# A hybrid conv/S5 layer on one core: state-space loads placed behind named weight loads, the conv matmuls, gelu and LayerNorm at other slots

## The chip, the cores and the metric

One core of a Trainium2 chip runs the whole kernel. The metric is the time of one launch in microseconds on the device. TensorE is called PE here, VectorE DVE, ScalarE ACT, GpSimd POOL, SyncE SP. "SPq" is SP's instruction queue, which issues nearly all DMAs; POOL issues the rest.

## The reference, cut to what matters

One layer is computed for 256 new positions of one sequence and 8 positions of each of 8 samples, 320 tokens together, in float32.

```python
xn = rmsnorm(x, norm_mix)
proj = xn @ w_in                        # 2048 -> 3072: value, gate, s_in of 1024 each
u = c_val * sigmoid(c_gate)             # group A
up = concat([conv_buf, u])              # conv_buf: the 30 rows kept of each sample
y = depthwise_conv(up, conv_w) + conv_b # width 31, then LayerNorm over channels, silu
# group B: S5, 64 groups of 16 channels, 64 complex states each
hs = associative_scan(complex, bu)      # starts from the incoming state of each sample
y = Re(C hs) + D * u; y = gelu(y); y = y * sigmoid(y @ w_glu)
mix = concat([rmsnorm(yc), rmsnorm(ys)]) @ w_out
h = x + mix
h = h + (silu(hn @ w_ffn_gate) * (hn @ w_ffn_up)) @ w_ffn_down
```

The outputs are the final rmsnorm of h for both kinds of token, the last 30 conv input rows and the last S5 states.

## The kernel before, in words

**The main work.** Every product with a weight matrix runs as three matmuls on rounded parts: weight and activation are each split into hi and lo, and hi*hi, lo*hi and hi*lo are added up in PSUM. The weights pass through in 352 sub-units (subs). A sub is two blocks of 128 weight rows by 512 columns, which makes 24 matmuls of 128x128 on 320 columns (two row blocks, four column blocks, three products; lines 151 to 153). `emit_dma` (line 113) loads its 512 KB into one of 4 `raw` buffers, in one DMA for the S5 columns and in two of 256 KB where value and gate columns are taken together. `emit_prep` (line 122) makes `hi` on ACT (line 127) and `lo` on DVE (line 128); `lo` is the last reader, so it frees the raw buffer, and the load of sub i waits for `lo` of sub i-4. Subs 0 to 15 are the S5 part of the input projection, 16 to 47 its conv part, 48 to 55 the S5 GLU, 56 to 87 the output projection (the S5 half first, then the conv half), and the rest is the FFN.

**What sets the order.** The program is written out sub by sub, and every piece is written under `when(slot)`: the slot, in units of subs, is a priority, and a scheduler puts each engine's instructions into one fixed order from these priorities and its own model of when operands are ready. `run_slot(i)` (line 132) writes the load of sub i at slot i-9, the split at i-2 and the matmuls at i. All other work of the mixer is a table, `PLAN`, of (what, index, slot):

```python
P_POST = [24, 25.5, 27, 28.5, 30, 31.5, 33, 34.5]
P_CONV = [27, 30, 35, 34, 43, 42, 51, 54]
+ [("gelu", b, P_GELU + b / 2) for b in range(8)]
+ [("conv", b, P_CONV[b] - (0 if b in V_CONV else 2.2)) for b in range(8)]
```

On each engine the instructions then run strictly in that order. A DMA is an instruction of SP's queue as well: while it waits for a buffer, all that stands behind it on SP waits too.

**The conv.** `conv_chunk(c)` (line 357) handles 128 channels. It loads the samples' old rows `stn` into its only buffer (line 361), turns them on PE (line 368) and copies them beside the new rows in `ubuf`; it turns the rows that are kept (line 371), copies them to `uo` and stores them as outputs 2 and 5 (lines 374, 375); then four DMAs copy four shifted views of `ubuf` into `ub` (line 381), 316 KB each. At slot `P_CONV[c]` PE runs 32 matmuls on 256 columns (line 389) and 32 on 64 columns (line 393); the trace counts each of these float32 matmuls twice. Chunks 3 and 5 do their taps on DVE instead. `gelu`, `ln_mean` to `ln_end` (slots `P_GELU` and `P_LN`) follow; LayerNorm closes with the row factors that the conv half of the output projection needs (`rg` line 292, turned on PE at line 300, then `Rc` line 302 and `t` line 993).

**The S5 part.** `s5_load2` (line 471), called from `s5_params2` (line 579) at slot 4, issues the B matrices `braw` (lines 475, 476), the C matrices `cn` (477, 478) and the incoming states `ssn` (482), ahead of them a zero fill of the scratch `KTd` (588), and `load_taps` the conv taps `cwn` (237). `post` (line 1182) reads a Toeplitz tile `tst` back from `KTd` through POOL, makes `hbd` on ACT, and on PE runs 8 matmuls of line 803 and 8 of line 808 (16 and 16 as the trace counts them), whose result is stored to `yd` (814); `gelu` reads `yd` back as `yl` (842), eight DMAs for each half. The copy of the 22 rows of old conv state that output 5 keeps is one DMA (1191).

Of the kernel before, what the change touches and what calls it, by code (L numbers as in the profile page):

```python
# [8 lines left out]
F32 = mybir.dt.float32  # L9
F32R = mybir.dt.float32r  # L10
I32 = mybir.dt.int32
AF = mybir.ActivationFunctionType
# [11 lines left out]
P_CONV = [27, 30, 35, 34, 43, 42, 51, 54]  # L24
V_CONV = {3: 0.2, 5: 0.2}
P_GELU = 44
P_LN = 62
E_AT = {2: 0, 3: 1024}
PT_BUFS = 2
N_CBLK = 1  # L30

# [14 lines left out]
        + [("copy", 0, 65)])  # L46
# [8 lines left out]
PREP_AHEAD = 2  # L55
@with_exitstack
def kernel(ctx: ExitStack, tc: tile.TileContext,
# [46 lines left out]
    raws = {}  # L104
    hls = {}
# [7 lines left out]
    def emit_dma(i):  # L113
        g, k0 = subs[i]
        r = rawp.tile([128, 2, 512], F32, tag="raw", name="raw")
        for w, row0, col0, n, off in g.srcs:
            SP.dma_start(r[:, :, off:off + n],
                         w[row0 + k0 * 128:row0 + (k0 + 2) * 128, col0:col0 + n]
                         .rearrange("(k p) n -> p k n", p=128))
        raws[i] = r  # L120

# [10 lines left out]
    def run_slot(i):  # L132
        with when(i - DMA_AHEAD):
            emit_dma(i)
# [65 lines left out]
    def sm_tile(shape, name):  # L200
        return s5.tile(shape, F32, name=name, tag="sm", bufs=4)
# [33 lines left out]
    def load_taps():  # L235
        late["cwn"] = s5.tile([128, 1024], F32, tag="ww", name="cwn", bufs=VW)
        SP.dma_start(late["cwn"][:31], conv_w[0])
# [118 lines left out]

    def conv_chunk(c):
        u = us_.pop(c)
        traced.add(("conv", c))
        stn = convp.tile([120, 2, 128], F32, name="stn", bufs=1)  # L360
        SP.dma_start(stn, sc_dram[:, c * 128:(c + 1) * 128]
                     .rearrange("(h r) c -> r h c", h=2))
# [108 lines left out]
    def s5_load2():  # L471
        braw = s5.tile([128, 2, 32, 16], F32, tag="et", name="braw", bufs=ET)
        cn = [s5.tile([128, 8, 64], F32, name=f"cn{i}", tag="ww" if i else "et", bufs=VW if i else ET)
              for i in range(2)]
        SP.dma_start(braw[:, 0], ssm_B_re[0].rearrange("(q g) p c -> (g p) q c", g=2))
        SP.dma_start(braw[:, 1], ssm_B_im[0].rearrange("(q g) p c -> (g p) q c", g=2))
        SP.dma_start(cn[0], ssm_C_re[0].rearrange("(k g) c p -> (g c) k p", g=8))
        SP.dma_start(cn[1], ssm_C_im[0].rearrange("(k g) c p -> (g c) k p", g=8))
        stn = [[sm_tile([128, 128], f"ssn{r}{h}") for h in range(2)] for r in range(2)]
        for r, src in enumerate((state_ssm_re, state_ssm_im)):  # L480
            for h in range(2):
                SP.dma_start(stn[r][h], src[0].rearrange("b (q g) p -> b q (g p)", g=2)
                            [:, 16 * h:16 * h + 16, :])
        return braw, cn, stn
# [94 lines left out]
    def s5_params2():  # L579
# [3 lines left out]
        for c in Cblk:  # L583
# [4 lines left out]
        SP.dma_start(KTd[:, 8:15].rearrange("b s c n -> (s c) b n"),  # L588
                     z[:, None, :].to_broadcast([112, 8, 128]))
        braw, cn, stn = s5_load2()  # L590
# [22 lines left out]
        for r in range(2):  # L613
            ps = sx_tile([128, 2, 128])
            for h in range(2):
                T.transpose(ps[:, h, :], stn[r][h], ident)
            A.activation(st0[:, r].rearrange("p (h q) b -> p h b q", h=2),
                         ps.rearrange("p h (b q) -> p h b q", b=8), AF.Copy)
# [530 lines left out]
    with when(-1.5):  # L1149
        load_x(4)  # L1150
        load_params()
    x_block(0)
# [18 lines left out]

    def c_step(c):
        return c
# [8 lines left out]
    def post(b):  # L1182
# [6 lines left out]
                  cw=conv_weights, conv=conv_chunk, sample=lambda b: s5_sample_states(),  # L1189
                  states=lambda b: s5_states(), open_g=lambda b: open_g(),  # L1190
                  copy=lambda b: SP.dma_start(ncv_s[0, :, 0:22, :], state_conv[0, :, 8:30, :]))
# [66 lines left out]
```

## Time and profile before

| | before |
|---|---|
| median of 3 runs | 1426.7 us (1422.41 to 1427.59) |
| the profiled execution's own time | 1431.02 us |
| its span | 1428.9 us |
| PE busy | 1385.4 us, 97% of the span |
| DVE busy | 827.2 us, 58% |
| ACT busy | 554.1 us, 39% |
| mean granted PE clock over the span | 0.982 |
| DMA | 220.11 MB, 154 GB/s on average |

A granted clock of 1.00 is PE at 2.4 GHz, 0.50 is 1.2 GHz. In a row of the timeline the columns are the start in us, the time to the end of the last of the merged instructions, the engine and line, the operation, what it writes and reads, how many, and in brackets the idle time of the engine before them and what ended it. Matmuls overlap, so a stretch of them is measured from start to start.

### The profile page before, as it was taken

What the parts mean: (1) busy time and instruction counts of PE and PEld (TensorE: products, weight loads), DVE (VectorE), ACT (ScalarE), POOL (GpSimd) and SP (SyncE); (2) the same over time, 40 slices, a digit from 0 to 9 for tenths busy, and PEclk for the clock granted to TensorE, in tenths of its full rate; (3) what the DMA queues carried; (4) which work ended last, traced back from release to release, by engine and by line L of the source; (5) the groups of instructions that cost most, each with busy time, mean ns of one, the idle gap of its engine ahead of it and who ended that gap; (6) DMA issues with size and microseconds to landing.
All of it is one profiled execution on the core that took longest, in us unless ns stands there. A gap on an engine that the chain in (4) does not pass through costs nothing.

```text
span 1428.9 us, 24831 instructions
## 1 busy us (share of the span) xinstructions
PE 1385.4 (97%) x10226; PEld 1352.4 (95%) x10226; DVE 827.2 (58%) x1518; ACT 554.1 (39%) x807; POOL 30.3 (2%) x61
## 2 busy tenths in 40 slices
PE   9899997899999999999999999999999999999995
PEld 8899986888999999999999999999999999999995
DVE  6788998776887744435434444443444435444465
ACT  7434433355364433333333332333333233332232
POOL 0121010000000000000000000000000000000000
PEclk9999998999999999999999999999999999999998
DMA  8875565467443444444444444445444444454432
GB/s 243 224 163 143 161 166 169 124 133 220 161 160 108 159 141 149 154 148 148 150 152 154 149 148 148 148 148 157 153 148 148 148 149 149 156 181 148 148 133 74
DMA packets 146585, 220.11 MB, mean 154 GB/s; under 512 B 32377, under 2 KB 57529, under 8 KB 146328
## 3 DMA queue, kind: packets, MB, share of 16 engines
q1 hardware_dynamic: 143336, 208.50, 47.3%
q0 software_dynamic: 3136, 10.03, 2.9%
q8 instruction: 80, 1.31, 0.4%
q14 instruction: 33, 0.27, 0.1%
HBM read 201.04 MB, written 10.41 MB: 148 GB/s over the span
## 4 chain that ended last, share of the span: by engine, by line
PE 88%; DMA 5%; DVE 2%; SPq 2%; ACT 1%; issue 1%; ACTq 0%; DVEq 0%
PE mm L151 27%; PE mm L152 27%; PE mm L153 27%; DMA ub<-ubuf 2%; PE cx L389 2%; DMA raw<-in_w_in_dram 2%; DVE lo L128 1%; SPq L842 1%; SPq L381 1%; ACT hi L127 1%; PE sx L808 1%; PE sx L710 1%; DMA yl<-yd 0%; DMA stn<-in_state_conv_dram 0%; PE sx L803 0%
## 5 line engine op out<-in xcount | busy, mean ns | idle before, releaser
L128 DVE TENSOR_TENSOR lo<-raw,hi 128x1024 fp32r<-128x1024 f32 x352 | 430.4, 1224 | 439.8 <-ACT hi L127 439.4
L127 ACT ACTIVATE hi<-raw 128x1024 fp32r<-128x1024 f32 x352 | 372.4, 1059 | 670.7 <-PE mm L152 605.2
L151 PE MATMUL mm<-hn,hi 128*128 128x320 f32 x1408 | 434.7, 309 | 0.0
L152 PE MATMUL mm<-hn,hi 128*128 128x320 f32 x1408 | 434.6, 309 | 0.0
L153 PE MATMUL mm<-hn,lo 128*128 128x320 f32 x1408 | 431.0, 309 | 0.0
L151 PEld LDWEIGHTS mm<-hn,hi 128*128 128x128 f32 x1408 | 264.2, 188 | 0.1
L152 PEld LDWEIGHTS mm<-hn,hi 128*128 128x128 f32 x1408 | 264.3, 188 | 0.0
L153 PEld LDWEIGHTS mm<-hn,lo 128*128 128x128 f32 x1408 | 263.2, 188 | 0.0
L151 PE MATMUL mm<-aout,hi 128*128 128x320 f32 x704 | 217.4, 309 | 0.0
L152 PE MATMUL mm<-aout,hi 128*128 128x320 f32 x704 | 217.1, 309 | 0.0
L153 PE MATMUL mm<-aout,lo 128*128 128x320 f32 x704 | 214.7, 309 | 0.0
L152 PEld LDWEIGHTS mm<-aout,hi 128*128 128x128 f32 x704 | 132.2, 188 | 0.0
L151 PEld LDWEIGHTS mm<-aout,hi 128*128 128x128 f32 x704 | 132.2, 188 | 0.0
L153 PEld LDWEIGHTS mm<-aout,lo 128*128 128x128 f32 x704 | 131.5, 188 | 0.0
L151 PE MATMUL mm<-xhl,hi 128*128 128x320 f32 x384 | 117.8, 321 | 5.4 <-ACT hi L127 4.3
L152 PE MATMUL mm<-xhl,hi 128*128 128x320 f32 x384 | 121.1, 318 | 0.3 <-DVE xhl L258 0.3
L153 PE MATMUL mm<-xhl,lo 128*128 128x320 f32 x384 | 120.9, 318 | 0.4 <-DVE lo L128 0.4
L151 PEld LDWEIGHTS mm<-xhl,hi 128*128 128x128 f32 x384 | 72.1, 192 | 7.7 <-ACT hi L127 4.5
L152 PEld LDWEIGHTS mm<-xhl,hi 128*128 128x128 f32 x384 | 73.5, 192 | 1.5 <-DVE xhl L258 0.9
L153 PEld LDWEIGHTS mm<-xhl,lo 128*128 128x128 f32 x384 | 73.2, 191 | 1.8 <-DVE lo L128 0.7
L1072 DVE TENSOR_TENSOR h<-mm,h 128x320 f32<-128x320 f32 x64 | 30.0, 488 | 41.1 <-PE mm L153 41.1
L389 PE MATMUL cx<-ub,cw 128*32 128x256 f32 x384 | 33.8, 467 | 16.0 <-DMA ub<-ubuf 16.0
(314 smaller groups left out, 1384.5 us busy)
## 6 DMA issues: line engine op xcount, KB each, us to landing
raw<-in_w_ffn_gate_dram SPq DMA_DIRECT2D x88, 512.0 KB
raw<-in_w_ffn_up_dram SPq DMA_DIRECT2D x88, 512.0 KB
raw<-in_w_ffn_down_dram SPq DMA_DIRECT2D x88, 512.0 KB
raw<-in_w_in_dram SPq DMA_DIRECT2D x64, 256.0 KB
raw<-in_w_out_dram SPq DMA_DIRECT2D x32, 512.0 KB
raw<-in_w_in_dram SPq DMA_DIRECT2D x16, 512.0 KB
ub<-ubuf SPq DMA_DIRECT2D x24, 316.0 KB
tst<-KTd POOLq DMA_DIRECT2D x8, 512.0 KB, 5.3
```

The source lines that it names most:

```text
L127: A.activation(hi, src, AF.Copy)
L128: V.tensor_tensor(lo, src, hi.bitcast(F32), op=OP.subtract)
L151: T.matmul(ps, wh, xh, start=(k == 0), stop=False)
L152: T.matmul(ps, wh, xl, start=False, stop=False)
L153: T.matmul(ps, wl, xh, start=False, stop=(k == g.nk - 1))
L381: SP.dma_start(ub[:, b, :], bass.AP(tensor=u.tensor, offset=u[32 * b:32 * b + 32].offset, ap=[[u.ap[0][0], 32], [8, 4], [1, UW - 24]]))
L389: T.matmul(acc[32 * b:32 * b + 32, 0:256], cw[:, b, k, :], ub[:, b, k:k + 256], start=(k == 0), stop=False, skip_group_check=True)
L710: T.matmul(ps[64 * g2:64 * g2 + 64, q, r, :], e[:, q, r, 64 * g2:64 * g2 + 64], uall[:, 8 * b + 2 * q + g2, :], start=True, stop=True)
L808: T.matmul(ps[:, g, :], t2[:, g].rearrange("p t c -> p (t c)"), uall[:, 8 * b + g, :], start=False, stop=(g == 7), skip_group_check=True)
L842: SP.dma_start(yls[16 * g:16 * g + 16], bass.AP(tensor=yd.tensor, offset=yd.offset + b * 128 * NTOK + 40 * g, ap=[[NTOK, 16], [16 * NTOK, ...
L1072: V.tensor_tensor(h[:, n, :], ps, h[:, n, :], op=OP.add)
```

## The change

The order of the work is changed, not the arithmetic. Line numbers of the changed kernel are up to 24 higher than those above; the matmuls of the conv, for example, are lines 406 and 410 there.

- The loads of the first 16 subs are written ahead of all other work (with the same slots as before), so that others can name them. `behind(i)` puts what it encloses behind the load of sub i on SP: the B matrices behind sub 8, the C matrices behind 9, the taps behind 11, the zero fill behind 13, the copy of old conv rows behind 60.
- The incoming states become a job of their own at slot 13.5, their transposes at 15.5.
- The `stn` loads become jobs at `P_CONV - 6`, with two buffers instead of one.
- Conv chunks 0, 1, 2, 4 and 7 get slots later by 0.6, 1, 0.6, 0.6 and 0.5. Their copies into `ub` are placed relative to the same slots.
- gelu goes from slot 44 to 40 (the eight follow at half-slot steps), LayerNorm from 62 to 58, the copy of old rows from 65 to 62.

```diff
-P_CONV = [27, 30, 35, 34, 43, 42, 51, 54]
+P_CONV = [27.6, 31, 35.6, 34, 43.6, 42, 51, 54.5]
 V_CONV = {3: 0.2, 5: 0.2}
-P_GELU = 44
-P_LN = 62
+P_GELU = 40
+P_LN = 58
 E_AT = {2: 0, 3: 1024}
...
 N_CBLK = 1
+P_STATE = 13.5
...
         + [("conv", b, P_CONV[b] - (0 if b in V_CONV else 2.2)) for b in range(8)]
-        + [("copy", 0, 65)])
+        + [("stn", b, P_CONV[b] - 6) for b in range(8)]
+        + [("incoming", 0, P_STATE), ("copy", 0, 62)])
 P_RMIX = 0.58
...
 PREP_AHEAD = 2
+FIRST_SUBS = 16
+B_BEHIND, C_BEHIND, TAPS_BEHIND, ZERO_BEHIND, COPY_BEHIND = 8, 9, 11, 13, 60
 @with_exitstack
...
     raws = {}
+    issues = {}
     hls = {}
...
         for w, row0, col0, n, off in g.srcs:
-            SP.dma_start(r[:, :, off:off + n],
-                         w[row0 + k0 * 128:row0 + (k0 + 2) * 128, col0:col0 + n]
-                         .rearrange("(k p) n -> p k n", p=128))
+            issue = SP.dma_start(r[:, :, off:off + n],
+                                 w[row0 + k0 * 128:row0 + (k0 + 2) * 128, col0:col0 + n]
+                                 .rearrange("(k p) n -> p k n", p=128))
         raws[i] = r
+        issues[i] = issue.ins
+    def behind(i):
+        return tc.issue_after(issues[i])
...
     def run_slot(i):
-        with when(i - DMA_AHEAD):
-            emit_dma(i)
+        if i not in issues:
+            with when(i - DMA_AHEAD):
+                emit_dma(i)
         with when(i - PREP_AHEAD):
...
         late["cwn"] = s5.tile([128, 1024], F32, tag="ww", name="cwn", bufs=VW)
-        SP.dma_start(late["cwn"][:31], conv_w[0])
+        with behind(TAPS_BEHIND):
+            SP.dma_start(late["cwn"][:31], conv_w[0])
...
+    stn_ = {}
+    def conv_states(c):
+        stn_[c] = convp.tile([120, 2, 128], F32, name="stn", bufs=2)
+        SP.dma_start(stn_[c], sc_dram[:, c * 128:(c + 1) * 128]
+                     .rearrange("(h r) c -> r h c", h=2))
     def conv_chunk(c):
...
         traced.add(("conv", c))
-        stn = convp.tile([120, 2, 128], F32, name="stn", bufs=1)
-        SP.dma_start(stn, sc_dram[:, c * 128:(c + 1) * 128]
-                     .rearrange("(h r) c -> r h c", h=2))
+        stn = stn_.pop(c)
         win_ = u[:, 350:654].rearrange("p (b t) -> p b t", t=38)
...
               for i in range(2)]
-        SP.dma_start(braw[:, 0], ssm_B_re[0].rearrange("(q g) p c -> (g p) q c", g=2))
-        SP.dma_start(braw[:, 1], ssm_B_im[0].rearrange("(q g) p c -> (g p) q c", g=2))
-        SP.dma_start(cn[0], ssm_C_re[0].rearrange("(k g) c p -> (g c) k p", g=8))
-        SP.dma_start(cn[1], ssm_C_im[0].rearrange("(k g) c p -> (g c) k p", g=8))
-        stn = [[sm_tile([128, 128], f"ssn{r}{h}") for h in range(2)] for r in range(2)]
-        for r, src in enumerate((state_ssm_re, state_ssm_im)):
-            for h in range(2):
-                SP.dma_start(stn[r][h], src[0].rearrange("b (q g) p -> b q (g p)", g=2)
-                            [:, 16 * h:16 * h + 16, :])
-        return braw, cn, stn
+        with behind(B_BEHIND):
+            SP.dma_start(braw[:, 0], ssm_B_re[0].rearrange("(q g) p c -> (g p) q c", g=2))
+            SP.dma_start(braw[:, 1], ssm_B_im[0].rearrange("(q g) p c -> (g p) q c", g=2))
+        with behind(C_BEHIND):
+            SP.dma_start(cn[0], ssm_C_re[0].rearrange("(k g) c p -> (g c) k p", g=8))
+            SP.dma_start(cn[1], ssm_C_im[0].rearrange("(k g) c p -> (g c) k p", g=8))
+        return braw, cn
...
         G.memset(hbd, 0.0)
-        SP.dma_start(KTd[:, 8:15].rearrange("b s c n -> (s c) b n"),
-                     z[:, None, :].to_broadcast([112, 8, 128]))
-        braw, cn, stn = s5_load2()
+        with behind(ZERO_BEHIND):
+            SP.dma_start(KTd[:, 8:15].rearrange("b s c n -> (s c) b n"),
+                         z[:, None, :].to_broadcast([112, 8, 128]))
+        braw, cn = s5_load2()
...
                                  AF.Copy, scale=-1.0 if r else 1.0)
-        for r in range(2):
-            ps = sx_tile([128, 2, 128])
+    def s5_incoming():
+        stn = [[sm_tile([128, 128], f"ssn{r}{h}") for h in range(2)] for r in range(2)]
+        for r, src in enumerate((state_ssm_re, state_ssm_im)):
             for h in range(2):
-                T.transpose(ps[:, h, :], stn[r][h], ident)
-            A.activation(st0[:, r].rearrange("p (h q) b -> p h b q", h=2),
-                         ps.rearrange("p h (b q) -> p h b q", b=8), AF.Copy)
+                SP.dma_start(stn[r][h], src[0].rearrange("b (q g) p -> b q (g p)", g=2)
+                            [:, 16 * h:16 * h + 16, :])
+        with when(P_STATE + 2):
+            for r in range(2):
+                ps = sx_tile([128, 2, 128])
+                for h in range(2):
+                    T.transpose(ps[:, h, :], stn[r][h], ident)
+                A.activation(st0[:, r].rearrange("p (h q) b -> p h b q", h=2),
+                             ps.rearrange("p h (b q) -> p h b q", b=8), AF.Copy)
...
         load_params()
+    for i in range(FIRST_SUBS):
+        with when(i - DMA_AHEAD):
+            emit_dma(i)
     x_block(0)
...
+    def copy_rows(b):
+        with behind(COPY_BEHIND):
+            SP.dma_start(ncv_s[0, :, 0:22, :], state_conv[0, :, 8:30, :])
     def c_step(c):
...
     parts_ = dict(v=pool_v, pre=pre, e=s5_e, w=pool_w, scan=s5_scan, post=post, gelu=gelu,
-                  cw=conv_weights, conv=conv_chunk, sample=lambda b: s5_sample_states(),
+                  stn=conv_states, cw=conv_weights, conv=conv_chunk, sample=lambda b: s5_sample_states(),
+                  incoming=lambda b: s5_incoming(),
                   states=lambda b: s5_states(), open_g=lambda b: open_g(),
-                  copy=lambda b: SP.dma_start(ncv_s[0, :, 0:22, :], state_conv[0, :, 8:30, :]))
+                  copy=copy_rows)
     for what, b, prio in sorted(PLAN, key=lambda x: x[2]):
```

**SP, the start of the program.** The rows run from the C matrices `cn` to the load of sub 9; `raw` with 128x2x512 is the load of a sub, `braw` and `cn` are the B and C matrices, `ssn` the incoming states, `xTd` stores of the normalised input.

Before:

```order
L477 DMA cn_489<-in_ssm_C_re_dram 128x8x64
L478 DMA cn_490<-in_ssm_C_im_dram 128x8x64
L117 DMA raw<-in_w_in_dram 128x2x512
L482 DMA ssn_495<-in_state_ssm_re_dram 128x1x128
L482 DMA ssn_496<-in_state_ssm_re_dram 128x1x128
L263 DMA xTd<-convy 128x320 x2
L482 DMA ssn_497<-in_state_ssm_im_dram 128x1x128
L237 DMA cwn<-in_conv_w_dram 31x1024
L361 DMA stn<-in_state_conv_dram 120x2x128
L263 DMA xTd<-convy 128x320
L482 DMA ssn_498<-in_state_ssm_im_dram 128x1x128
L117 DMA raw<-in_w_in_dram 128x2x512
```

Changed:

```order
L373 DMA stn<-in_state_conv_dram 120x2x128 x2
L122 DMA raw<-in_w_in_dram 128x2x512
L493 DMA braw<-in_ssm_B_re_dram 128x32x16
L494 DMA braw<-in_ssm_B_im_dram 128x32x16
L275 DMA xTd<-convy 128x320 x3
L122 DMA raw<-in_w_in_dram 128x2x512
L496 DMA cn_521<-in_ssm_C_re_dram 128x8x64
L497 DMA cn_522<-in_ssm_C_im_dram 128x8x64
```

Before, the zero fill, both `braw` and both `cn` stand ahead of the load of sub 8, and `ssn`, `cwn` and `stn` between the loads of 8 and 9. Changed, the load of sub 8 is ahead of `braw`, that of sub 9 ahead of `cn`, and the four `ssn` have gone from here; they stand some 16 loads later.

**PE, conv chunk 0.** L803 and L808 (changed: L827, L832) are the two halves of a `post`, each row of the order counting a matmul as one instruction.

Before:

```order
L803 MATMUL sx<-hbd,ww 128x82 x8
L368 MATMUL sx<-ident,stn 128x120 x2
L389 MATMUL cx<-ub,cw 32x256 x12
L808 MATMUL sx<-us,t_2328 128x41
L389 MATMUL cx<-ub,cw 32x256
L808 MATMUL sx<-us,t_2328 128x41
L389 MATMUL cx<-ub,cw 32x256
L808 MATMUL sx<-us,t_2328 128x41
```

Changed:

```order
L832 MATMUL sx<-us,t_2330 128x41 x8
L406 MATMUL cx<-ub,cw 32x256 x32
L410 MATMUL cx<-ub,cw 32x64 x32
L827 MATMUL sx<-hbd,ww 128x82 x8
L832 MATMUL sx<-us,t_2399 128x41 x8
L385 MATMUL sx<-ident,stn 128x120 x2
```

Before, the second half of a `post` is dealt out one by one between the conv's matmuls (eight times in all); changed, it is through before the conv, whose matmuls stand together.

**SP ahead of conv chunks 2 and 4, and PE ahead of chunk 2.** `ub` are the four copies that a conv's matmuls read, `yl` the read-back for gelu, `yd` the stores of `post`.

Before, SP ahead of chunk 2:

```order
L814 DMA yd<-y_2600 128x320
L361 DMA stn<-in_state_conv_dram 120x2x128
L381 DMA ub<-ubuf_111 128x1x632 x2
L814 DMA yd<-y_2667 128x320
L381 DMA ub<-ubuf_111 128x1x632 x2
```

Changed, SP ahead of chunk 2:

```order
L838 DMA yd<-y_2671 128x320
L373 DMA stn<-in_state_conv_dram 120x2x128
L398 DMA ub<-ubuf_111 128x1x632 x2
L838 DMA yd<-y_2785 128x320
L398 DMA ub<-ubuf_111 128x1x632 x2
```

Changed, PE just ahead of chunk 2:

```order
L827 MATMUL sx<-hbd,ww 128x82 x5
L388 MATMUL sx<-ident,ubuf_112 94x128
L827 MATMUL sx<-hbd,ww 128x82 x3
L832 MATMUL sx<-us,t_2979 128x41 x8
L406 MATMUL cx<-ub,cw 32x256
```

Changed, SP ahead of chunk 4:

```order
L373 DMA stn<-in_state_conv_dram 120x2x128
L795 DMA out_dram<-so_3070 8x16x128
L122 DMA raw<-in_w_glu_dram 128x2x512
L398 DMA ub<-ubuf_111 128x1x632
L866 DMA yl<-yd 16x32x40 x4
L122 DMA raw<-in_w_glu_dram 128x2x512
L866 DMA yl<-yd 16x32x40 x4
```

The `stn` row ahead of chunk 2 is now the load for chunk 5. It goes into the buffer of chunk 3's rows, so it waits until PE has transposed those, and PE does that 13 sub matmuls and one whole `post` ahead of conv 2. The `stn` row ahead of chunk 4 is the load for chunk 6, which waits for the transposes of chunk 5's rows, 4.08 subs ahead of conv 4 on PE; behind it come one of the four `ub` copies, eight `yl`, three sub loads and two stores before the other three `ub` copies. Before, the eight `yl` stood behind the last `ub`.

## Rows read from the trace of the kernel before

**Rows 1.** Busy time by stretches: length, PE, PEld, DVE, ACT, POOL, granted clock, DMA.

```profile
50.89:57.72 6.83, 5.07 (x19) 5.07 (x20) 3.04 (x7) 1.70 (x3) 0.00 (x0) 0.50 0.88 276
218.14:221.55 3.41, 3.41 (x40) 2.07 (x36) 3.41 (x10) 0.76 (x2) 0.00 (x0) 0.50 0.08 27
242.04:248.86 6.82, 3.65 (x35) 1.77 (x38) 5.18 (x17) 1.75 (x3) 0.00 (x0) 0.50 0.88 268
298.00:314.00 16.00, 13.12 (x73) 11.85 (x72) 16.00 (x33) 11.38 (x26) 0.00 (x0) 0.89 0.43 120
433.18:440.00 6.82, 6.15 (x23) 6.16 (x24) 6.29 (x16) 3.58 (x8) 0.00 (x0) 0.50 0.00 0
444.50:480.00 35.50, 35.50 (x245) 35.50 (x244) 30.41 (x51) 19.57 (x31) 0.00 (x0) 1.00 0.47 164
```

**Rows 2.** Who waited for whom, PE, 46 to 440 us: total us, times, longest.

```profile
PE cx L389 <- DMA ub<-ubuf: 16.0, 6, 4.2
...
PE mm L153 <- DVE lo L128: 1.6, 4, 0.7
...
PE mm L152 <- DVE gehl L855: 0.9, 1, 0.9
PE sx L300 <- DVE rg L292: 0.7, 1, 0.7
PE sx L368 <- DMA stn<-in_state_conv_dram: 0.6, 1, 0.6
```

**Rows 3.** Timeline of PE, 50 to 60 us.

```profile
52.65 0.63 PE L151 MATMUL mm<-xhl,hi 128*128 128x320 f32 x1 [4.27 <-ACT hi L127]
...
58.34 1.86 PE L605 MATMUL sx<-ident,cn 128*64 128x128 f32 x30
```

**Rows 4.** Timeline of PE at the six convs; two of 24 rows at chunk 0.

```profile
193.84 1.51 PE L389 MATMUL cx<-ub,cw 128*32 128x256 f32 x24 [0.64 <-DMA ub<-ubuf]
...
204.70 0.31 PE L371 MATMUL sx<-ident,ubuf 128*94 128x128 f32 x1
...
217.66 4.71 PE L389 MATMUL cx<-ub,cw 128*32 128x256 f32 x52 [4.10 <-DMA ub<-ubuf]
...
245.21 4.14 PE L389 MATMUL cx<-ub,cw 128*32 128x256 f32 x38 [4.17 <-DMA ub<-ubuf]
...
330.74 5.34 PE L389 MATMUL cx<-ub,cw 128*32 128x256 f32 x64 [2.51 <-DMA ub<-ubuf]
...
347.93 3.67 PE L389 MATMUL cx<-ub,cw 128*32 128x256 f32 x64 [0.68 <-DMA ub<-ubuf]
```

**Rows 5.** Chain that ended last, 180 to 250 us: issues, landings, conv and post.

```profile
184.29 0.67 SPq L381
...
187.88 5.92 DMA ub<-ubuf
...
210.27 7.26 DMA ub<-ubuf
...
223.02 0.95 PE cx L393 x51
...
224.90 1.75 PE sx L803 x16
226.65 1.77 PE sx L808 x16
...
239.21 5.96 DMA ub<-ubuf
```

**Rows 6.** Chain that ended last, 40 to 54 us: start, us, what.

```profile
36.24 5.47 DMA raw<-in_w_in_dram
...
42.89 8.54 DMA raw<-in_w_in_dram
```

**Rows 7.** Timeline of SP's queue, 24 to 50 us.

```profile
28.44 4.74 SPq L476 DMA_DIRECT2D braw<-in_ssm_B_im_dram  x1
```

**Rows 8.** Timeline of DVE, 20 to 53 us.

```profile
28.05 1.23 DVE L128 TENSOR_TENSOR lo<-raw,hi 128x1024 fp32r<-128x1024 f32 x1
```

## The prediction, written before the changed kernel had run

> **What bounds the kernel now.** PE is the engine to read: 352 subs of 24 matmuls, and at full clock one matmul starts every 0.145 us (245 in 35.50 us, last row of [rows 1]). A gain can only be time in which PE stands still or runs at half clock, so I looked for both, in this order. First the waits of PE between 46 and 440 us, where the mixer runs [rows 2]: most of it is the conv waiting for its `ub` copies, 16.0 us in six waits, then come small ones on DVE; ahead of them, at 52.65 us, lies one of 4.27 us for a `hi` [rows 3]. Behind 440 us PE stands as in the last row of [rows 1], busy for all of 35.50 us, so the FFN gives nothing. Then the stretches at granted clock 0.50, the 1.2 GHz level [rows 1]: each follows an idle time, and costs half of what PE was busy in it. The stretch of 3.41 us behind chunk 1 has its like behind chunk 4, at 310 us in gelu, and behind chunk 6; each costs 1.7 us. Then, for each wait, what ended it.
>
> **What each place loses now.**
> - Sub 9: PE is idle from 48.38 to 52.65 [rows 3]. 2.5 us of that lie ahead of the half-clock stretch at 50.89, and that lasts 6.83 us for 19 matmuls, which are worth 2.8 at full clock. Lost: 2.5 + 4.0 = 6.5 us.
> - Chunk 0: idle 0.64, and from its first matmul to the next other work 10.86 us (193.84 to 204.70) [rows 4]. Alone a conv takes 3.67 + 0.95 = 4.6 us [rows 4, 5], and the half `post` dealt out between takes 1.77 when it stands alone [rows 5]. Lost: 0.64 + 10.86 - 4.6 - 1.8 = 5.1.
> - Chunk 1: 4.10 + 1.7 = 5.8. Chunk 2: 4.17 + half of 3.65 = 6.0. Chunk 6: 2.51 + 1.7 = 4.2. Chunk 7: 0.7. Chunk 4 has what is left of the 16.0: 3.9, + 1.7 = 5.6.
> - gelu: 1.6 + 0.9 + 0.6 waiting for `lo`, `gehl` and a `stn`, + 1.7 = 4.8. DVE is busy for all 16.00 us of 298 to 314 [rows 1].
> - LayerNorm: 0.7 for `rg`, and half of 6.15 us at half clock = 3.8.
>
> Together 42.5 us; that is all the change can reach.
>
> **Part by part, what stays of them.**
>
> *S5 loads behind named loads.* The load of sub 9 is issued at 42.89 and needs 8.54 us [rows 6], because `braw` (one issue holds SP for 4.74 us, [rows 7]), `cn`, `ssn` and others stand ahead of it. Its buffer is free at 28.05 + 1.23 = 29.3 [rows 8], so SP alone is late. In the new order the second `braw` issue, at 28.44 before, has two `stn` and the load of 8 ahead of it in place of the zero fill, about 1 us more; it ends near 34, and three `xTd` later sub 9 goes out near 36 and lands at 41.5 to 44.5, with the 5.47 and 8.54 us of [rows 6]. `hi` takes no longer than the 1.23 of `lo`, and PE wants it at 48.4: early enough. I take 0.5 us as the rest, bounds 0 and 6.5. The moved loads must not be missed: `cn` goes out 4 us later, near 37 to 40, and its transposes run on PE at 58.34 [rows 3], or 52 with the stall gone; even 8.54 us of landing is in time. The zero fill is first needed when a `post` reads `tst`; `cwn`, `ssn` (four issues between loads that run ahead) and the copy of old rows have nobody waiting. These I cost at nothing; if sub loads were the bound in the mixer they would cost their issue time, some 4 us.
>
> *Conv matmuls later.* Chunk 0 now starts after that half `post`, 1.8 us later, which covers its 0.64, and stands together: nothing stays. Chunk 1 starts 1.9 subs later (6.6 us), and the two stores that held its last `ub` copy back come behind it. Both together are more than the 4.10 it waits; but the `post` just ahead of it hangs on DVE's scan: 2.0 stays, bounds 0 and 5.8. Chunk 7: nothing stays.
>
> Chunk 2 is the doubtful one. SP must now wait for PE's transposes of chunk 3 before it can issue `ub`, and PE has just 13 matmuls (1.9 us) and a `post` (1.75 + 1.77, [rows 5]) to run from there: 5.4 us. SP issues `stn`, three `ub` and a `yd` at some 0.67 us each [rows 5] ahead of the last copy, 3.4 us, and that lands 5.96 us later [rows 5]: PE waits 9.4 - 5.4 = 4.0, + 1.7 at half clock = 5.7. No gain to speak of; bounds 0 and 9.5 + 1.7.
>
> Chunk 4 is similar: 4.08 subs of cover (14.4 us) from the transposes on which SP waits; behind them 18 issues at 0.67 (12 us) and 6 us of landing: 3.6 + 1.7 = 5.3 stays. Bounds 0 (its eight `yl` may be issued faster) and 11.2. Chunk 6's `ub` no longer has gelu's work on DVE ahead of it: 0.5 stays, bounds 0 and 4.2.
>
> A rule of the Trainium skill bears on the last two (DMA: Bandwidth & Descriptors, Anatomy of one DMA): there a DMA issued by POOL costs 2.0 us and its bytes at 436 GB/s. An estimate by that page is 2.7 us for a `ub` copy, and the waits of chunks 2 and 4 would be 3 us shorter each. The three last copies of [rows 5] took 5.92, 7.26 and 5.96 us, so I go by the rows.
>
> *gelu up by four.* `yl` is issued before `ub` of chunk 4 is done rather than after, and gelu's DVE pieces come out of the crowded 298 to 314: 0.5 stays, bounds 0 and 4.8.
>
> *LayerNorm up by four.* The column sums ahead of `rg` move up by half a sub (2 us), more than the 0.7. The later wait of PE for `t` stays, but is too short to be alone followed by a slow stretch, as the 0.7 of chunk 7 was not [rows 4]. 0.8 stays, bounds 0 and 3.8.
>
> **Sum.** Left: 0.5 + 0 + 2.0 + 5.7 + 5.3 + 0.5 + 0 + 0.5 + 0.8 = 15.3 of 42.5, a gain of 27 us. Against the profiled execution's 1431.0 us that is 1404; this execution is 4.3 above the median, so the forecast for the median is 1426.7 - 27 = **1400 us**.
>
> **The rivals.**
>
> 1. *All `ub` waits go.* If copies land faster once `out` stores and sub loads do not crowd them, chunks 1, 2 and 4 lose nothing: 13 us more, 1387. For it: chunks 0 and 7 waited just 0.64 and 0.68 [rows 4]. Against: none of the shown last copies took under 5.9 us, and SP's wait ahead of chunk 2 stands in the order.
>
> 2. *Half of it.* Chunks 1 and 6 wait as before (3.8 and 3.7 lost) and LayerNorm keeps its slow stretch (3.0): 1400 + 10.5 = 1410.5. For it: each conv's matmuls and its copies move by the same slots, so much of the distance is unchanged, and PE arrives earlier by what it gained before. A rest of sub 9's wait belongs here too: if its load still drains behind `braw`, it needs over 11.3 us from issue to landing before PE waits. The Trainium skill says (DMA: Bandwidth & Descriptors, Queues, rings and completion order) that each DMA engine consumes descriptors in ring order; by that rule the load is not free of the small pieces of `braw` just because SP issued it. The load of 8, directly behind `cn`, landed in 5.47 [rows 6], so I give this rest little.
>
> 3. *DVE becomes the bound.* Its whole order is fixed, and it has stretches without a gap [rows 1]. If scan, `post` and gelu follow DVE alone, what PE gains up to 300 us (sub 9 6, chunk 0 5.1, chunk 1 3.8, gelu 4.3) returns as waits for `lo` and `hbd`: about 8 us are left, 1419. Against: of PE's waits only 3 to 4 us name DVE [rows 2].
>
> 4. *Slower: SP's waits for `stn` buffers expose the copies.* A `stn` load now stands in SP's queue ahead of copies that have nothing to do with it, and waits for PE. If at chunks 1, 2, 4 and 6 SP is let go only as PE reaches the conv, each waits the whole path from first issue to last landing, 9.5 us (184.29 to 193.80, [rows 5]), + 1.7: 45 against 21.6 now. That loses 23; `yl`, behind the same waits, keeps gelu's 4.8; sub 9, chunk 0, LayerNorm and chunk 7 still give 15: 1435. It decides where PE's cover falls under about 2 us; in the order it is 5.4 and 14.4 at the two places that I looked at.
>
> That the change does nothing can be left out: on SP, PE and DVE the order is another.
>
> **How the numbers follow.** A measurement of this kernel can tell 0.5%, 7.1 us, from no change: faster is under 1419.6. Forecast (1394 to 1406) 0.48; rival 1 (1384 to 1394) 0.20; rival 2 (1406 to 1415) 0.20; rival 3 (1415 to 1424) 0.08, a third of it still faster; rival 4 0.04, most of it slower. Range: 1385 to 1414, which leaves out rivals 3 and 4 and the best of rival 1. Faster 0.90, within 0.5% 0.07, slower 0.03.
>
> **What would show it.** Right: no wait of PE for a `hi` near 50 us and no slow stretch there; conv 0 without a break, in 4.6 us; waits for `ub` left at chunks 2 and 4, some 4 us each with a slow stretch; PE's waits for `gehl` gone; full clock at 430 us. Wrong: `ub` waits at all five chunks (rival 2 or, at 9 us, rival 4), at none (rival 1), or long waits for `lo` or `hbd` (rival 3).

## The result, and the profile after

| | before | changed |
|---|---|---|
| median | 1427.1 us (4 runs, 1422.4 to 1429.0) | 1407.5 us (4 runs, 1404.3 to 1408.8) |
| ratio to before | | 0.9864, 95% interval 0.9844 to 0.9884 |
| own time of the profiled execution, span | 1431.02 us, 1428.9 us | 1407.77 us, 1405.9 us |
| mean granted PE clock | 0.982 | 0.987 |

The change is 19.4 us faster (16.6 to 22.3). The forecast was 27 us, 1400, with a range to 1414: the direction and the range hold, the size is about three quarters. The spans of the two profiled executions differ by 23.0 us, mostly because the one of before was a slow one among its runs, by the 4.3 us that the prediction took off.

Who waited for whom on PE in the changed kernel, 40 to 440 us (total, times, longest), against [rows 2]:

```profile
PE cx L406 <- DMA ub<-ubuf: 7.6, 4, 4.2
PE sx L388 <- DVE ubuf L968: 2.0, 1, 2.0
PE mm L162 <- DVE t L1017: 1.1, 1, 1.1
PE mm L162 <- DVE vt L960: 0.4, 1, 0.4
...
```

The conv's waits have halved, the `hi` wait of sub 9 is gone, so are those for `gehl` and `rg`. One is new: 2.0 us for a `ubuf`. The stretches at half clock (length, PE, PEld, DVE, ACT, POOL, granted clock, DMA), and the place of sub 9:

```profile
211.59:221.83 10.24, 10.24 (x75) 7.63 (x78) 10.14 (x27) 3.27 (x7) 0.88 (x1) 0.50 0.50 162
279.85:286.68 6.83, 5.64 (x56) 3.12 (x60) 6.63 (x15) 1.84 (x5) 0.00 (x0) 0.50 1.22 168
300.33:303.75 3.42, 3.41 (x13) 3.15 (x14) 3.42 (x8) 1.24 (x3) 0.00 (x0) 0.50 0.76 202
46.00:58.00 12.00, 12.00 (x118) 11.09 (x117) 10.24 (x30) 5.21 (x11) 4.08 (x7) 1.00 0.91 288
```

There are three where there were seven, but the first is longer than any before. PE's timeline at chunks 0, 1, 2, 4, 6 and 7:

```profile
188.14 3.69 PE L406 MATMUL cx<-ub,cw 128*32 128x256 f32 x64
...
210.18 0.63 PE L406 MATMUL cx<-ub,cw 128*32 128x256 f32 x4 [2.06 <-DMA ub<-ubuf]
210.74 2.96 PE L827 MATMUL sx<-hbd,ww 128*128 128x82 f32 x16
213.49 3.55 PE L832 MATMUL sx<-us,t 128*128 128x41 f32 x16
216.97 5.81 PE L406 MATMUL cx<-ub,cw 128*32 128x256 f32 x58
...
242.91 0.62 PE L406 MATMUL cx<-ub,cw 128*32 128x256 f32 x2 [0.67 <-DMA ub<-ubuf]
...
281.04 6.42 PE L406 MATMUL cx<-ub,cw 128*32 128x256 f32 x64 [4.21 <-DMA ub<-ubuf]
...
312.19 3.69 PE L406 MATMUL cx<-ub,cw 128*32 128x256 f32 x64
...
330.69 3.67 PE L406 MATMUL cx<-ub,cw 128*32 128x256 f32 x64 [0.66 <-DMA ub<-ubuf]
```

Counted as the prediction counted (idle, and half of what PE was busy in at half clock):

| place | before | predicted to stay | measured |
|---|---|---|---|
| sub 9 | 6.5 | 0.5 | 0 |
| chunk 0 | 5.1 | 0 | 0 |
| chunk 1 | 5.8 | 2.0 | 2.06 + 5.1 = 7.2 |
| chunk 2 | 6.0 | 5.7 | 0.67 + 0.2 = 0.9 |
| chunk 4 | 5.6 | 5.3 | 4.21 + 2.8 = 7.0 |
| gelu | 4.8 | 0.5 | 2.0 + 1.7 = 3.7 |
| chunks 6 and 7 | 4.9 | 0.5 | 0.7 |
| LayerNorm | 3.8 | 0.8 | 0.2 |
| sum | 42.5 | 15.3 | 19.7 |

42.5 - 19.7 = 22.8 us, which is the 23.0 by which the spans differ. So the account by places closes for these two profiles (the medians are 19.4 apart); the question is why chunks 1 and 4 and gelu kept more, and chunk 2 less, than I thought.

### The profile page after: what moved, and what is told of

Same layout as the page of the kernel before. It is cut to its first block, busy times and chain, and to the rows that moved or that the text cites. A ratio compares the mean times of both kernels' runs of the same rounds, so it can differ in the third digit from the quotient of the medians.

```text
span 1405.9 us, 24845 instructions
## 1 busy us (share of the span) xinstructions
PE 1376.3 (98%) x10226; PEld 1347.1 (96%) x10226; DVE 826.3 (59%) x1518; ACT 554.9 (39%) x807; POOL 30.3 (2%) x61
## 4 chain that ended last, share of the span: by engine, by line
PE 81%; DMA 2%; DVE 1%; ACT 0%; SPq 0%; issue 0%; ACTq 0%
PE mm L162 26%; PE mm L164 26%; PE mm L163 26%; PE cx L406 1%; DMA ub<-ubuf 1%; PE sx L832 0%; PE sx L827 0%; DMA yl<-yd 0%; SPq L398 0%; DMA stn<-in_state_conv_dram 0%; DMA tst<-KTd 0%; PE cx L410 0%; PE sx L1137 0%; DVE lo L138 0%; PE sx L312 0%; PE sx L320 0%
## 5 line engine op out<-in xcount | busy, mean ns | idle before, releaser
L434 DVE SCALAR_TENSOR_TENSOR convy<-ubuf,convw,convy 128x256 f32<-128x256 f32 (+1 forms) x120 | 41.2, 378 | 1.6 <-ACT convy L430 0.9
```

The costliest lines, as they stand in the source:

```text
L434: V.scalar_tensor_tensor(dst, src(k), convw[:, c, k:k + 1], dst, op0=OP.mult, op1=OP.add)
```

## The experiments

Each time stands against the kernel before on the same chip, as a ratio with its 95% interval. A difference between two such ratios is uncertain by some 4 to 5 us. Each trace is of one execution.

### One part alone

Theory: the parts add up. Rival: what PE gains early is lost again to DVE or at the next wait. The kernel before got the S5 part alone (all edits of the change with these undone):

```diff
-P_CONV = [27.6, 31, 35.6, 34, 43.6, 42, 51, 54.5]
+P_CONV = [27, 30, 35, 34, 43, 42, 51, 54]
-P_GELU = 40
+P_GELU = 44
-P_LN = 58
+P_LN = 62
-        + [("stn", b, P_CONV[b] - 6) for b in range(8)]
...
-        stn = stn_.pop(c)
+        stn = convp.tile([120, 2, 128], F32, name="stn", bufs=1)
+        SP.dma_start(stn, sc_dram[:, c * 128:(c + 1) * 128]
...
```

> The kernel before with the S5 part of the change alone: loads of the first 16 subs written first, B, C, taps, zero fill and copy behind named loads, incoming states as their own job. Parts add up (my reading of the two traces): only the wait at sub 9 and its half-clock stretch go, 6.5 us of 1427.1, so about 1420.5; the conv waits stay at 16 us. Rival, DVE sets the pace behind it: the 6.5 us come back as other waits up to 200 us, and the time stays within 2 us of 1427.

Measured: 1421.42 us, 0.9979 (0.9963 to 0.9995): 3.0 us, not 6.5. Sub 9's wait is gone in the trace. Two waits of PE at 292 and 295 us are new, where before had waits of 1.6 us for `lo` in all:

```profile
PE mm L161 <- ACT hi L136: 2.5, 1, 2.5
PE mm L163 <- DVE lo L137: 2.3, 2, 2.1
```

They do not account for the missing 3.5 us: the conv's waits in this trace are 12.9 us instead of 16.0, up to 200 us hardly anything has come back, and by stages (table below) it loses 8.8 us less than the trace of before. Why the medians differ by only 3.0 is not shown.

Then the conv slots and `stn` jobs alone, added to the kernel before:

```diff
-P_CONV = [27, 30, 35, 34, 43, 42, 51, 54]
+P_CONV = [27.6, 31, 35.6, 34, 43.6, 42, 51, 54.5]
...
+        + [("stn", b, P_CONV[b] - 6) for b in range(8)]
...
-        stn = convp.tile([120, 2, 128], F32, name="stn", bufs=1)
...
+        stn = stn_.pop(c)
```

> The kernel before with the conv slots and the stn jobs alone. Parts add up: chunk 0 stands together (5 us) and chunk 2 waits under 1 us without a slow stretch (5 us), chunk 1 keeps a wait and a slow stretch through the post behind it (0 to -1.5), chunk 4 as before or better since gelu's loads are not ahead of its copies (0 to 5): 1413 to 1419. Rival (conv gains need the PE to be early or the S5 loads out of the way): above 1422.

Measured: 1421.95, 0.9969 (0.9950 to 0.9987): 4.4 us. The conv waits fell from 16.0 to 6.3 us as hoped, but those for a `stn` load and for `rg` grew (the 5.9 for `hi` is sub 9, which this part leaves alone); PE's waits in this run:

```profile
PE cx L395 <- DMA ub<-ubuf: 6.3, 4, 1.9
PE mm L152 <- ACT hi L128: 6.3, 2, 5.9
PE sx L374 <- DMA stn<-in_state_conv_dram: 4.1, 1, 4.1
PE sx L301 <- DVE rg L293: 1.8, 1, 1.8
```

And gelu and LayerNorm alone:

```diff
-P_GELU = 44
+P_GELU = 40
-P_LN = 62
+P_LN = 58
```

> The kernel before with gelu at slot 40 and LayerNorm at 58 alone. If they add up: waits in gelu with their slow stretch (4.8) and the slow stretch at LayerNorm (3.8) go: 1418.5. If gelu's read-backs ahead of chunk 4's copies cost what the change shows there (chunk 4 lost 7.6 in it, 5.6 before): 1420.5, with a wait of 4 to 6 us at chunk 4. Rival: gelu's waits only move, under 4 us gained, 1423 or more.

Measured: 1423.89, 0.999 (0.997 to 1.001): nothing that can be told from zero. Chunk 4 waited 2.1 us, not the 4 to 6 of my condition. Together the three come to 3.0 + 4.4 + 1.4 = 8.8 us; the change has 19.4. **The parts do not add up.** They give more together than alone, by more than the intervals allow, which none of my rivals had.

### One part left out

The change with the S5 loads back where they stood before (the `ssn` loads and the other uses of `behind` go back with them):

```diff
-B_BEHIND, C_BEHIND, TAPS_BEHIND, ZERO_BEHIND, COPY_BEHIND = 8, 9, 11, 13, 60
-        + [("incoming", 0, P_STATE), ("copy", 0, 62)])
+        + [("copy", 0, 65)])
...
-        with behind(B_BEHIND):
-            SP.dma_start(braw[:, 0], ssm_B_re[0].rearrange("(q g) p c -> (g p) q c", g=2))
+        SP.dma_start(braw[:, 0], ssm_B_re[0].rearrange("(q g) p c -> (g p) q c", g=2))
...
-    for i in range(FIRST_SUBS):
-        with when(i - DMA_AHEAD):
-            emit_dma(i)
```

> The change without its S5 part. Parts add up: 1407.5 + 6.5 = 1414, with the wait for hi near 50 us back. Rival (the S5 gain is eaten later): 1408 to 1409, the same as the change.

Measured: 1406.65, 0.9880 (0.9854 to 0.9906): 17.1 us without the S5 part, 19.4 with it; the intervals overlap. The rival held nearly. This run also says which parts need each other: the conv part and the gelu and LayerNorm part gave 4.4 and 1.4 us alone and give 17.1 together, without the S5 part.

The change with gelu alone back at its old slot:

```diff
-P_GELU = 40
+P_GELU = 44
```

> The change with gelu at slot 44 as before. By my sum gelu's move is worth 4.3 us: 1411.8, with waits for gehl and lo between 290 and 310 us. Rival (as in the runs of parts alone, where gelu and LayerNorm moved alone gave nothing): within 2 us of 1407.5, since chunk 4's wait goes for what gelu loses.

Measured: 1415.46, 0.9924 (0.9898 to 0.9949). Gelu's slot is worth 8.6 us here (19.4 - 10.8), twice my 4.3. PE's waits in this run, 40 to 440 us:

```profile
PE cx L406 <- DMA ub<-ubuf: 6.8, 4, 2.2
PE sx L385 <- DMA stn<-in_state_conv_dram: 5.6, 1, 5.6
PE sx L312 <- DVE rg L304: 1.8, 1, 1.8
```

The wait moved from the conv to a `stn` load, as in the run with the conv slots alone, and LayerNorm's `rg` is late although its slot is the new one.

The change with LayerNorm alone back:

```diff
-P_LN = 58
+P_LN = 62
```

> The change with LayerNorm at slot 62 as before; on SP nothing moves. By my sum LayerNorm's move is worth 3 us: 1410.5, with a wait of 0.7 us or more for rg and a half-clock stretch of 6.8 us near 410 us. Rival: the conv slots alone had made LayerNorm worse (waits of 0.95, 1.78 and 1.11 us and 10.24 us at half clock in the run of the conv part alone), so it is worth 7 to 8: 1414.5 to 1415.5.

Measured: 1412.48, 0.9898 (0.9872 to 0.9925): LayerNorm's slot is worth 4.9 us, between my 3 and the rival's 7 to 8, and hardly outside the uncertainty. A wait of 2.0 for `rg` is back, and a half-clock stretch of 6.83 us behind it.

And the change with the old conv slots, its `stn` jobs kept:

```diff
-P_CONV = [27.6, 31, 35.6, 34, 43.6, 42, 51, 54.5]
+P_CONV = [27, 30, 35, 34, 43, 42, 51, 54]
```

> The change with the conv slots as before; the stn jobs, S5, gelu and LayerNorm parts stay. If the parts add up, the conv slots are worth what the run of the conv part alone showed (2 to 3 us): 1410. Theory after the runs so far: the parts work only together, since the conv slots free chunks 0 to 2 (13.8 us lost before, 8.1 in the change), and gelu's and LayerNorm's slots keep that from being lost again between 262 and 442 us; without the conv slots chunks 0 to 2 lose some 12 us and conv 0 is split by its post again (4.5): 1417 to 1422.

Measured: 1418.39, 0.9955 (0.9940 to 0.9970). The conv slots are worth 13.0 us in the change and 4.4 (with the `stn` jobs) alone. PE's first row has all of the old wait back:

```profile
PE cx L406 <- DMA ub<-ubuf: 15.9, 6, 4.0
```

What PE loses by stage (idle, and half of its busy time at half clock; chunk 0's split is the `post` dealt out between its matmuls), from one profile each, in us:

| kernel | sub 9 | chunk 0 split | chunks 0 to 2 | chunk 4 to 7, gelu, GLU | LayerNorm |
|---|---|---|---|---|---|
| before | 6.8 | 4.5 | 12.4 | 15.1 | 5.1 |
| S5 alone | 0 | 4.5 | 12.2 | 14.7 | 3.7 |
| conv alone | 7.9 | 0 | 7.7 | 13.7 | 7.6 |
| gelu and LayerNorm alone | 7.5 | 4.5 | 12.0 | 13.3 | 1.6 |
| the change without conv slots | 0 | 4.5 | 12.1 | 14.2 | 1.6 |
| without gelu | 0 | 0 | 7.7 | 15.2 | 6.8 |
| without LayerNorm | 0 | 0 | 7.2 | 11.1 | 8.1 |
| without S5 | 4.3 | 0 | 3.9 | 9.5 | 1.3 |
| the change | 0 | 0 | 8.1 | 11.4 | 1.3 |

One profile is not a measurement of a stage: conv alone and without S5 have the same order on every engine up to 262 us, and still differ by 3.6 us at sub 9 and by 3.8 at chunks 0 to 2. So compare them where their orders differ, behind chunk 2: there conv alone loses 4.2 us more from chunk 4 to the GLU and 6.3 more at LayerNorm. My reading is that the conv slots empty the stretch up to chunk 2 but push DVE's and SP's work behind it, and so pay only where the later slots make room for them; no run isolates that. The S5 part pays its 4 to 8 us at sub 9; what it costs at chunks 0 to 2 is the next question.

### Why the S5 part is worth so little

PE's timeline at chunk 1 in the run without the S5 part:

```profile
213.47 0.63 PE L395 MATMUL cx<-ub,cw 128*32 128x256 f32 x4 [1.09 <-DMA ub<-ubuf]
214.39 2.01 PE L809 MATMUL sx<-hbd,ww 128*128 128x82 f32 x16 [0.29 <-ACT hbd L799]
216.24 1.92 PE L814 MATMUL sx<-us,t 128*128 128x41 f32 x16
218.09 3.44 PE L395 MATMUL cx<-ub,cw 128*32 128x256 f32 x58
```

PE reaches it 4.3 us later (212.38 against 208.12), waits 1.09 instead of 2.06, stays at full clock, and starts conv 2 1.2 us ahead of the change (241.72 against 242.91). Of these 5.5 us, 1.0 is the shorter wait; the half-clock stretch, which this run does not have, costs the change 5.1.

That the S5 part is what brings the stretch is not shown, though. The run with the conv part alone has no S5 part either, and up to here it has the order of this run on every engine:

```profile
216.40 0.62 PE L395 MATMUL cx<-ub,cw 128*32 128x256 f32 x4 [1.84 <-DMA ub<-ubuf]
217.23:227.47 10.24, 10.24 (x68) 8.19 (x71) 10.21 (x29) 3.35 (x8) 0.88 (x1) 0.50 0.41 124
```

It waits 1.84 us and has the whole stretch (second row, by stretches). Nor does PE come much nearer to the copies: from SP's first issue of the four to PE's arrival it is 8.8 us in the change (199.34 to 208.12), 9.3 in the run without the S5 part (203.10 to 212.38) and 9.1 with the conv part alone (205.50 to 214.56); to the conv's start it is 10.8, 10.4 and 10.9. With the S5 part the copies go out earlier as well, and less than a microsecond lies between a wait that has the stretch behind it (1.84) and one that has none (1.09).

Two tries to take the stretch away; first conv 1's matmuls as a job of their own, behind the `post`:

```diff
+        + [("cmm", 1, P_CONV[1])]
...
-        with when(P_CONV[c]):
+        with (tc.issue_after(late["post4"]) if c == 1 else when(P_CONV[c])), when(P_CONV[c]):
```

> The change with conv 1's matmuls placed behind the post that splits them now (PE runs post 4, 3.5 us, while the last ub copy lands). Theory: the S5 part's 6 us are real but are given back at chunk 1, where PE arrives earlier, waits 2.06 us and then runs post and conv through a half-clock stretch of 10.24 us. Then the wait and the stretch go, PE stands 5 to 7 us earlier at chunk 2, and the time is 1400.5 to 1403 unless it is lost again at chunk 4. Rival: the post is not ready before 210.7 us anyway (its hbd comes from ACT and DVE): PE waits 2 us for hbd, the slow stretch stays, 1406 to 1408.

PE's timeline at the `post` in this run:

```profile
209.24 2.17 PE L834 MATMUL sx<-hbd,ww 128*128 128x82 f32 x16 [1.32 <-ACT hbd L824]
```

And the stretch at half clock that follows it (busy time by stretches, columns as above):

```profile
210.96:217.78 6.82, 6.82 (x51) 5.13 (x54) 6.82 (x20) 3.15 (x7) 0.88 (x1) 0.50 0.54 180
```

The `post` is not ready before 209.2 (the rival), the stretch is 6.83 us, and conv 2 starts 3.1 us earlier than in the change. But this edit also reorders what comes later: `rg` waits 1.8 us with 10.24 us at half clock behind it, and the time is 1414.61, 0.9922 (0.9897 to 0.9948), worse by 8 us. The second try leaves the order of PE, ACT and DVE as it is and moves only two of the copies of chunk 1 to POOL:

```diff
-            SP.dma_start(ub[:, b, :],
+            (G if c == 1 and b >= 2 else SP).dma_start(ub[:, b, :],
```

> The change with two of chunk 1's four ub copies issued by POOL instead of SP; the order of PE, DVE and ACT is that of the change, word for word. Theory: the S5 part's gain is given back at chunk 1 by a wait of 2.06 us and a half-clock stretch of 10.24 us behind it (some 7 us). SP's last issue for chunk 1 comes 2 us earlier and the copies land by 208 us: no wait above 1 us at chunk 1, no half-clock stretch there, 1400 to 1402. Rival 1: a copy from POOL lands as late, the wait and the stretch stay: 1406 to 1409. Rival 2: the wait goes but the post behind it is not ready (hbd at 209 us, as in the run with conv 1 behind the post), the stretch stays at 6.8 us: 1404 to 1406.

> The change without its S5 part, with the same two copies on POOL; the rest of the order is that of the run without the S5 part. There chunk 1 waited 1.09 us without a half-clock stretch. Theory: at most 1 us is won here, 1405.5 to 1407, so that the S5 part is worth 4 to 6 us once chunk 1 does not give it back. Rival (the S5 part is worth nothing whatever chunk 1 does): the same time as the run beside it with the S5 part, within 1.5 us.

Measured: with the S5 part 1407.98, 0.9877 (0.9855 to 0.9900); without 1411.51, 0.9900 (0.9875 to 0.9925). Rival 1 held: counted from the first of the four issues, the last one starts after 2.3 us instead of 3.4 and the conv after 10.7 instead of 10.8. In the run with the S5 part, the chain of waits at POOL's last copy (start, us, engine):

```profile
202.75 0.55 POOL ub L398
203.31 8.26 DMA ub<-ubuf
```

PE's timeline behind it:

```profile
211.70 0.62 PE L406 MATMUL cx<-ub,cw 128*32 128x256 f32 x4 [1.95 <-DMA ub<-ubuf]
```

And its stretch at half clock:

```profile
212.23:222.47 10.24, 10.24 (x66) 8.48 (x68) 10.20 (x29) 3.42 (x8) 0.90 (x1) 0.50 0.40 126
```

This pair repeats what the first showed: at chunk 1 waits of 1.95 and 1.08 us, a half-clock stretch of 10.24 us and none, 6.0 us between the two ahead of it (209.75 and 215.75) and 0.5 at conv 2 (244.48 and 245.00). In three pairs (alone, and these two) the S5 part is worth 0.21%, 0.16% and 0.23%, 2.3 to 3.3 us of the 6.0 that I gave it. As a ratio to before only the first is clear of zero by itself; but the last pair ran on one chip, 1406.9 to 1409.5 us in five runs with the part against 1408.6 to 1414.0 in six without. That the stretch would go with the wait was not shown, for no run took the wait away.

### Chunk 4

The edit names chunk 4's last copy and puts `yl` behind it (for that the gelu jobs are written after chunk 4's, at their old priorities):

```diff
...
-            for g in range(8):
-                SP.dma_start(yls[16 * g:16 * g + 16],
+            with tc.issue_after(late["ub4"]):
+                for g in range(8):
+                    SP.dma_start(yls[16 * g:16 * g + 16],
```

> The change with gelu's read-backs yl behind the last ub copy of chunk 4 on SP. Theory: the eight yl and two sub loads among the ub copies cause chunk 4's wait of 4.2 us and its half-clock stretch; both go, -4 to -7.6 us, and gelu comes 3 to 5 us later, which may cost 0 to 4: 1400 to 1407. Rival: the copies are late because SP waits for PE's transposes: the wait stays above 3 us, 1407 to 1409.

Measured: 1415.10, 0.9926 (0.9903 to 0.9948). The cause was right, the time was wrong: chunk 4 waits 1.34 us with no slow stretch instead of 4.21, but all of 262 to 345 us reads

```profile
PE cx L408 <- DMA ub<-ubuf: 7.2, 3, 4.8
PE mm L163 <- DVE gehl L882: 1.9, 2, 1.6
PE sx L385 <- DMA stn<-in_state_conv_dram: 1.5, 1, 1.5
PE mm L162 <- ACT hi L137: 0.9, 1, 0.9
```

where the change had 4.9 us for `ub` and 2.0 for `ubuf`. The wait has gone to chunk 6 (4.84 us) and to gelu, which now comes late.

### A candidate

```diff
-            for k in range(8):
-                for b in (3, 2, 1, 0):
+            for bs in (((0, 1), (2, 3)) if c in (0, 1, 4) else ((3, 2, 1, 0),)):
+                for k in range(8):
+                    for b in bs:
```

> A candidate: the change with the matmuls of chunks 0, 1 and 4 in two halves, copies 0 and 1 first, so that a conv can start when two of its four copies have landed. LayerNorm's sums stay where the change has them (75.33 subs). Theory: chunks 1 and 4 lost 7.2 and 7.6 us in the change, waits of 2.1 and 4.2 with their half-clock stretches; starting on two copies takes 1 to 2 us off each wait and, where the wait falls to about 1 us, the stretch: 1398 to 1404. Rival: the new order puts conv 1 1.4 subs (5 us) earlier on PE, so the wait stays whatever the copies do: 1406 to 1412.

Measured: 1409.33, 0.9889 (0.9870 to 0.9908), the same as the change within the intervals. Waits and slow stretches between 180 and 442 us fell from 20.7 to 13.1 us (PE waits 6.5 us for `ub` in all), and the span is still 2.0 longer: PE itself works more, and other work is in another order. Chunk 4, in halves, and chunk 6, as ever, in this run, both at full clock:

```profile
278.46 5.62 PE L407 MATMUL cx<-ub,cw 128*32 128x256 f32 x56
283.71 0.31 PE L411 MATMUL cx<-ub,cw 128*32 128x64 f32 x4
...
312.34 3.69 PE L407 MATMUL cx<-ub,cw 128*32 128x256 f32 x64 [2.24 <-DMA ub<-ubuf]
315.80 1.18 PE L411 MATMUL cx<-ub,cw 128*32 128x64 f32 x64
```

5.25 us for 56 matmuls from start to start against 3.46 for 64. No run beats the change clearly; the run without the S5 part was its equal once, and 3.5 us behind it with two of chunk 1's copies on POOL in both.

## Why the prediction was right or wrong

**What bounds the kernel: right in the main.** All of the gain lies in PE's time up to 440 us; the two sums by place close to 0.2 us of the spans. But a gain is not only idle or half-clock time, as the prediction had it: 4.5 of the 22.8 us are chunk 0's split, where PE was busy at full clock throughout but took 10.9 us for what takes 6.4 when the conv and the half `post` stand apart. The stretch in the kernel before:

```profile
193.84:204.70 10.86, 10.86 (x145) 6.01 (x146) 9.73 (x30) 3.04 (x7) 0.82 (x1) 1.00 0.43 134
```

**S5 loads: the wait as forecast, the worth half.** The load of sub 9 was to go out near 36. SP's queue in the timeline of the changed kernel, the loads of subs 8 and 9 (start, us to issue, tile<-source):

```profile
27.84 0.44 SPq L122 DMA_DIRECT2D raw<-in_w_in_dram  x1
...
36.07 0.41 SPq L122 DMA_DIRECT2D raw<-in_w_in_dram  x1
```

The wait and its slow stretch are gone, nothing waits for `cn`, and the rule of the Trainium skill that I set beside rival 2 (DMA: Bandwidth & Descriptors, Queues, rings and completion order) took nothing from it: `hi` was in time behind all of `braw`. What failed is the sum: I added sub 9's 6.0 us to gains behind it as if PE's lead lasted, and the pairs of runs give 2.3 to 3.3. In two pairs of traces the lead shrinks at chunk 1, with its half-clock stretch; where the part stands alone, the trace shows no such loss. Where the rest goes stays open.

**Chunk 0: right**, 4.6 us without a break. **Chunk 1: the term was mis-sized**, 2.0 against 7.2. The wait is the 2 us that I took, but by luck: I took it for a `post` that waits for DVE, and let a start 6.6 us later cover the copies. The copies moved with it. SP before, then changed, and in the last row the last copy as it lands:

```profile
204.85 1.23 SPq L381 DMA_DIRECT2D ub<-ubuf  x2
206.17 1.63 SPq L374 DMA_DIRECT2D out_dram<-uo  x1
...
199.34 5.36 SPq L398 DMA_DIRECT2D ub<-ubuf  x4
202.76 7.28 DMA ub<-ubuf
```

From the first issue to PE's arrival it is 8.7 us before (204.85 to 213.56) and 8.8 in the change (199.34 to 208.12). What shortened the wait is that the two stores no longer stand among the issues: the last one starts 3.4 us behind the first instead of 5.4. The half-clock stretch behind the wait, which I left out, is 5.1. I had the price of such a stretch from a conv of dense matmuls (3.41 us); here a `post` of narrow matmuls follows, and it lasts three times as long.

**Chunk 2: wrong step.** I let SP wait for the transposes of chunk 3's rows. In the trace the `stn` load goes out at 231.45, just behind the pair of transposes of chunk 2's own rows, and not behind the next pair. The two pairs in the chain of waits of the changed kernel:

```profile
231.21 0.21 PE sx L385 x2
...
236.55 0.21 PE sx L385 x2
```

and SP's queue in its timeline:

```profile
231.45 0.36 SPq L373 DMA_DIRECT2D stn<-in_state_conv_dram  x1
```

Which of two buffers a load takes is not in the order, and I assumed that they alternate. The cover is 5 us longer, the wait 0.67, and the change has 4.8 us that I gave away. At chunk 4 it is the same (SP is let go at 258.98, and the cover is 17.9 us instead of 14.4), but there the 18 issues took 15.3 us to the start of the last, 0.85 each and not 0.67, and its copy 6.8 us to land: 7.0 stayed for 5.3. The estimate of 2.7 us for a copy, by the Trainium skill (DMA: Bandwidth & Descriptors, Anatomy of one DMA), was further off than the rows.

**gelu: mis-sized**, 0.5 against 3.7: the old waits went, and PE's transposes for chunk 6 now wait 2.0 us for a `ubuf` that DVE writes behind gelu's work, which the prediction had out of chunk 6's way. Leaving gelu where it was costs 8.6 us, though, so most of this part's worth is that it clears the way for LayerNorm and the `stn` loads, which I had not priced at all. **LayerNorm: right** in what goes; its worth, 4.9 us, is above my 3 because the conv slots had made it later.

**The rivals.** DVE as the bound and copies exposed by SP's waits did not come; nor did all `ub` waits go. By my own bounds the 1407.5 us lie outside the forecast (1394 to 1406, 0.48) and just inside rival 2 (1406 to 1415, 0.20). By its places it was not quite rival 2: chunk 1 kept its loss, but chunk 6's wait for `ub` and LayerNorm's slow stretch went, and chunk 4 and gelu made up the rest. Its reason, that a conv's matmuls and its copies move by the same slots and the distance stays, is what the trace shows at chunk 1.

## What to carry to other kernels

A kernel whose order a scheduler makes from slots has to be costed as a whole: here three parts gave 3.0, 4.4 and 1.4 us alone and 19.4 together, and local repairs (chunk 4's copies first, conv 1 behind its `post`) cost 8 us elsewhere. When a wait is removed early, follow PE to the next wait and ask who is late there, before adding the gain to the sum; a later slot covers a copy only if the copy does not move with it. Price a wait with what PE runs right behind it. And one trace does not tell what a change does to a stage: in two traces with the same order sub 9 lost 4.3 us and 7.9.

## What the runs showed of the hardware

- **The half-clock stretch depends on more than the wait.** At chunk 1, nine runs follow the wait with a `post` of 82- and 41-column matmuls: waits of 2.06, 1.95, 1.84, 1.79, 1.72 and 1.54 us each had 10.24 us at 1.2 GHz behind them, one of 1.32 had 6.83, two of 1.09 and 1.08 none. With the dense conv behind it, waits of 4.10, 4.11, 3.97 and 3.93 us had only 3.41. The dense conv does not always keep it short: at chunk 4 a wait of 4.21 us went with 6.83 in the change, one of 2.22 with none in the run with gelu's old slot. No run changed only what follows a wait, so the reason stays open.
- **Alternating between two column groups is slower than between four.** A conv matmul has 32 columns of weights and writes 32 of the 128 rows of its result; which 32 is its column group. These matmuls start every 0.054 us when four groups take turns (64 in 3.46 us) and every 0.094 us with two (56 in 5.25 us), at the same clock: a round of two groups takes 0.19 us, hardly less than the 0.22 of a round of four.
- **A copy issued by POOL was no quicker.** 316 KB took 8.26 us from its issue to landing, against 7.28 for SP's last one in the change, at chunk 1 in both.
